# Two blocks of a transformer on one core: other splits, other places for the list steps of the experts

## The chip, the cores and the metric

The kernel runs on one core of a Trainium2 chip. The metric is the device time of one execution in microseconds (us). PE is the matrix engine, ACT the scalar engine, DVE the vector engine, POOL is GpSimd, and SP only issues transfers here.

## What is computed

512 tokens of 1024 float32 numbers pass two blocks. The first is a token mixer (mLSTM and pooled windows) followed by a mixture of 32 experts, of which each token uses four. The second is a stick-breaking attention with spatial gating. This case is about the experts:

```
gate = xb @ w_gate[e] + b_gate[e]
up = xb @ w_up[e] + b_up[e]
gate = jnp.minimum(gate, SWIGLU_LIMIT)
up = jnp.clip(up, -SWIGLU_LIMIT, SWIGLU_LIMIT)
glu = gate * jax.nn.sigmoid(SWIGLU_ALPHA * gate)
return (glu * (up + 1.0)) @ w_down[e] + b_down[e]
```

Each result row is weighted by its token's softmax gate and added to the token's output. All three weight matrices of all 32 experts are read: 96 matrices of 4 MB.

## The kernel before

**Weights.** A matrix comes in four blocks of 256 rows, 1 MB each, tile `wr` (128x2048). SP loads them (`fetch`, L132), up to eight blocks ahead of their use (`DM`). A block is then split into two tiles of the fast float32 format: ACT casts `wh` (L145), DVE subtracts `wl = wr - wh` (L148). PE multiplies with both. A block whose number stands in `k.raw` (L263) isn't split: PE multiplies `wr` itself as plain float32, which takes it more time. `next_w` keeps the instructions of the splits four blocks ahead of the product that uses them (`LEAD`).

**Places.** The experts are sorted by load at run time and stand in 32 places (`WIDE`). A wide place takes 112 rows; its activations are split into `xh` and `xl` (after the up product `ah` and `al`), which makes three products of a split block. A narrow place takes 64 rows, with both parts side by side in 128 columns (`xs`, `as`), so that two products do. The halves of a narrow result are added afterwards: ACT copies one (`part`), DVE adds (`sg`, `u`, `y`). From place 2 to 29 narrow and wide places alternate, and 30 and 31 are narrow.

**Which blocks are raw.** In gate and up of a wide place the last of four blocks; in down of every place the last. For a raw block the last 256 activations are needed unsplit: ACT copies them out of PSUM into `raws` (wide L888, narrow L900).

**Order.** In the expert stage every engine's order is the order of the Python program. `place(s)` emits gate(s), the transposes of the activations of place s-1 (`aT`, by `parts_T`), up(s), the transposes of the gathered rows of s+1 (tile `xg`), the gather for s+2 and down(s-1). So the stage repeats in pairs of places, each with one stretch of three narrow products (down N, gate N, up N) and one of three wide ones (down W, gate W, up W). Below, a block is named by product and number: D0 to D3, G0 to G3 and U0 to U3 are those of a narrow stretch.

**Steps.** Work that may be done later is a list of functions, `todo`; `product` pops one after each block. `lists` makes the token lists of four places: four marks on DVE (L800), then `rest`, 16 small matmuls into the PSUM tile `pl` (L806) and six small DVE operations. It runs at place 1 and at every fourth place to 24. Of the seven runs, six stand in a narrow stretch like that of rows 6; the other narrow stretches of the repeated part, eight, have none. Near the end `places`, `gates_T` and the bias of down are such steps too. `gates_T` copies a tile `g` on DVE (L1148) and transposes it on PE (L1151).

Of the kernel before, what the change touches and what calls it, by code (L numbers as in the profile page):

```python
# [16 lines left out]
S, D, P = 512, 1024, 128  # L17
# [229 lines left out]
def weight_order(k):  # L247

    a = k.a
    def cols(w, c0, n=512):  # L250
        kt = min(2048 // n, w.shape[0] // P)
        return [w[r:r + kt * P, c0:c0 + n].rearrange("(a p) c -> p a c", p=P) for r in range(0, w.shape[0], kt * P)]

    def rows(n, s):
        def block(r):
            def src(k):
                w = a[n][k.expert(s)]
                w = w.rearrange("e r c -> (e r) c") if s >= 2 else w
                return w[r:r + 2 * P].rearrange("(a p) c -> p a c", p=P)

            return src

        k.raw.update({len(out) + D // P // 2 - 1} if n == "w_down" or WIDE[s] else ())  # L263
        out.extend(block(r) for r in range(0, D, 2 * P))

    out = cols(a["w_in"], 1024) + cols(a["w_in"], 2048, P)
    for c0 in (512, 0, 2056, 1536):
        out += cols(a["w_in"], c0)
    for c0 in (0, 512):
        out += cols(a["w_out"], c0)[::-1]  # L270
    for e in range(NE + 1):
        if e < NE:
            rows("w_gate", e)
            rows("w_up", e)
        if e:
            rows("w_down", e - 1)
    k.experts_end = len(out)
    for cs, up in ((1024, 0, 512, 2560, 2048, 1536, 3584, 4096), "w_up_a"), ((3072, 4608, 5120), "w_up_b"):
        for c0 in cs:
            out += cols(a["w_in_2"], c0)  # L280
        for c0 in (0, 512):
            out += cols(a[up], c0)
    for c0 in (0, 512):
        out += cols(a["w_out_2"], c0)
    return out
# [503 lines left out]
    return placed  # L789


def lists(k, places, entries, name, kinds, out, soon):


    nc, n, shp = k.nc, places.shape[2], [P, NTC, P]
    oh4 = k.b4("loh" if n == 1 else "oh4", (P, n, NTC, P), BF)

    def marks(e):
        slots = k.slots[:, kinds[e], None, :].to_broadcast(shp)
        nc.vector.tensor_tensor(oh4[:, e], slots, places[:, :, e, None].to_broadcast(shp), op=OP.is_equal)  # L800

    def rest():
        pt = k.bank("pl")
        for e in range(n):
            for c in range(NTC):
                nc.tensor.matmul(pt[:, 8 * e:8 * e + 5], oh4[:, e, c], entries[:, c, e], start=(c == 0), stop=(c == NTC - 1))  # L806
        L = pt[:, :8 * n].rearrange("p (e w) -> p e w", w=8)
        tok = k.small("tok" + name, [P, n], bufs=2)
        nc.vector.tensor_reduce(tok, L[:, :, :2], axis=X, op=OP.add)
        ti, tf, ga = (k.small(t + name, [P, n], dt, bufs=3) for t, dt in (("ti", I32), ("tf", F32), ("ga", F32)))  # L810
        for kind in sorted(set(kinds)):
            for odd in range(2):
                es = [e for e in range(odd, n, 2) if kinds[e] == kind]
                if es:
                    assert es == list(range(es[0], es[-1] + 1, 2))
                    es = slice(es[0], es[-1] + 1, 2)
                    rows_of(k, tok[:, es], ti[:, es], tf[:, es], kind)
        nc.vector.tensor_reduce(ga, L[:, :, 2:5], axis=X, op=OP.add)
        out.extend((ti[:, e:e + 1], ga[:, e:e + 1], tf[:, e:e + 1]) for e in range(n))

    for e in range(n):
        soon(lambda e=e: marks(e))
    soon(rest)


# [23 lines left out]
def moe(k):  # L849
# [7 lines left out]

    info = []

    def listed(n, soon):  # L860

        s0 = max(2, listed.n)
        listed.n = s0 + n
        ss = slice(s0, s0 + n)
        lists(k, k.posm_s[:, :, ss], k.entry_s[:, :, ss], "l%d" % n, [int(not WIDE[s]) for s in range(s0, s0 + n)], info, soon)

    listed.n = 0
    ti, tf, placed = first_rows(k)
# [2 lines left out]
    k.fetch(FW)  # L871
    k.depth = 9
    bias_g, bias_u = k.bias

    def raw_part(name, parity):

# [2 lines left out]
    def parts_T(src, name, parity, wide=True):  # L879


        if wide:
            hi, lo, raw = *(k.b4(name + n, (P, KD - 2, C), F32R) for n in "hl"), raw_part(name, parity)
            def use(k0, pt):
                n = min(4, KD - 2 - k0)
                k.ondve = k.hilo(pt[:, :n], hi[:, k0:k0 + n], lo[:, k0:k0 + n])
                if n < 4:
                    nc.scalar.copy(raw, pt[:, n:])  # L888

            k.transposes(src[:C], use)  # L890
            return hi, lo, raw
        x, pt = k.b4(name + "s", (P, KD, P), F32R), k.bank("tp", (P, KD, CS))
        for kk in range(KD):
            nc.tensor.transpose(pt[:, kk], src[:CS, kk * P:(kk + 1) * P], k.ident[:CS, :CS])  # L894
        if name == "x":
            k.hilo(pt, x[:, :, :CS], x[:, :, CS:])
            return x,
        k.hilo(pt[:, :KD - 2], x[:, :KD - 2, :CS], x[:, :KD - 2, CS:])
        raw = raw_part(name, parity)[:, :, :CS]
        nc.scalar.copy(raw, pt[:, KD - 2:])  # L900
        return x, raw

    def one_of(s):
        if s < 2:
# [4 lines left out]
        nc.vector.tensor_copy(one, k.sel[:, 1:, s:s + 1].to_broadcast([96, 2, CS]))  # L909
        return one.rearrange("p a c -> p (a c)")  # L910

    todo = []

    def product(xT, b, one, get):

        wide, raw = len(xT) == 3, xT[-1] if len(xT) > 1 else None
        p, n = k.bank2("pe"), C if wide else P
        for i in range(2 if b is not None else 0):
            nc.tensor.matmul(p[:n, i], one, b[:, i * 512:(i + 1) * 512], start=True, stop=False, skip_group_check=True)  # L919
        last = KD - 3 if raw is not None else KD - 1  # L920
        for k0 in range(0, KD, 2):
            w = get()
            for i in range(2):
                kk = k0 + i
                if len(w) == 1:
                    lr = (raw[:, i], w[0]),
                elif wide:
                    lr = (xT[0][:, kk], w[0]), (xT[0][:, kk], w[1]), (xT[1][:, kk], w[0])
                else:
                    lr = (xT[0][:, kk], w[0]), (xT[0][:, kk], w[1])  # L930
                for n_, (l, r) in enumerate(lr):
                    for j in range(2):
                        o = i * D + j * 512
                        nc.tensor.matmul(p[:l.shape[1], j], l, r[:, o:o + 512], start=(b is None and kk == 0 and n_ == 0),  # L934
                                         stop=(kk in (last, KD - 1) and n_ == len(lr) - 1), skip_group_check=True)
            if todo and not k.fixed:
                todo.pop(0)()
        return p[:n].rearrange("p a b -> p (a b)")

    lim = 7.0 / (1.0 + math.exp(-1.702 * 7.0))  # L940

    def soon(f):

        f() if k.fixed else todo.append(f)

    def added(p, name):

# [114 lines left out]
    listed(2, lambda f: f())  # L1062
    gather(xgs[0], info[2][0], C if WIDE[2] else CS)

    def place(s, u, xT, one):

        if s == 1 or s % 4 == 0 and s + 4 < NE:
            listed(4, todo.append)
        sg = gate(xT, one, k.next_w)
        aT = parts_T(u, "a", (s - 1) % 2, WIDE[s - 1])  # L1070
        u = up(sg, xT, one, k.next_w)
# [4 lines left out]
            gather(xgs[s % 2], info[s + 2][0], C if WIDE[s + 2] else CS)  # L1076
        if s < NE - 1:
            result(down(aT, k.next_w), *info[s - 1][:2])
        if s == NE - 3:
            todo.extend((lambda: places(k, [info[e][2] for e in (NE - 2, NE - 1)]), lambda: gates_T(k),  # L1080
                         lambda: bias(k, "b_down", 0.0, 3)))
        return u, xT, aT, one

    k.lead, k.depth, one = LEAD, DM, one_of(1)
    with tc.manual_schedule(engines=ALL_ENGINES):
        for s in range(1, LOOP_AT + 1):
            u, xT, aT, one = place(s, u, xT, one)
        while todo:
            todo.pop(0)()
    longer_lists()  # L1090
    with tc.manual_schedule(engines=ALL_ENGINES):
        for s in range(LOOP_AT + 1, NE):
            if s == NE - 2:
                k.stop = k.experts_end
            u, xT, aT, one = place(s, u, xT, one)
        aT1 = []
        todo.append(lambda: aT1.append(parts_T(u, "a", (NE - 1) % 2, WIDE[NE - 1])))
        k.depth = DE
        p = down(aT, k.next_w)
    k.lead = 0  # L1100
    with tc.manual_schedule(engines=IN_ORDER):
        before_last(k)
        k.depth = DE2
        k.ready += [k.parts() for _ in range(4 - len(k.ready))]
        ys = [weighted(p, info[NE - 2][1])]
        p = down(aT1[0], k.next_w)
        k.wv = [k.next_w()]
        ys.append(weighted(p, info[NE - 1][1]))
        later = []
# [31 lines left out]
        nc.vector.tensor_scalar(k.ohs[:, n], iof, tf, None, op0=OP.is_equal)  # L1141


def gates_T(k):

    nc, pg, g3 = k.nc, k.bank("pg3"), k.b4("g3", (P, NTC, 96))
    k.gT3 = k.b4("gT3", (96, S), F32R)
    nc.vector.tensor_copy(g3.rearrange("p c (r e) -> p c r e", r=3),  # L1148
                          k.pg[:, :, 1, None, :].to_broadcast([P, NTC, 3, NE]))
    for c in range(NTC):  # L1150
        nc.tensor.transpose(pg[:96, c * P:(c + 1) * P], g3[:, c], k.ident)  # L1151
    nc.scalar.copy(k.gT3, pg[:96])
# [328 lines left out]
```

## Time and profile before

| | |
|---|---|
| time, median of 3 runs | 1841.8 us (1838.49 to 1843.19) |
| the profiled execution, its own time | 1837.83 us, span 1836.1 us |
| PE, DVE, ACT, POOL busy | 93%, 70%, 55%, 13% of the span |
| expert stage | about 250 to 1393 us on the trace |
| four places (two pairs) in its middle | 139.9 to 140.0 us, four times in a row |

A busy time is a sum over stages. What a stage waits for is read from the timelines of its engines, where a number in brackets is the idle time ahead of an instruction and what ended it.

### The profile page before, as it was taken

The numbers are of one execution on the slowest core, as the hardware profiler recorded it, in microseconds if no ns is written. First come the engines' busy times: TensorE is split into PE (matmuls) and PEld (weight loads), VectorE is DVE, ScalarE is ACT, GpSimd is POOL, SyncE is SP. The second block draws the span as 40 slices with busy tenths as digits, with TensorE's granted clock in tenths as the row PEclk, the third lists the DMA queues.
The fourth block names the chain that finished last, engine by engine and source line by source line (L and its number), as shares of the span: only waits on it lengthen the run. The fifth ranks groups of instructions, "written<-read, shape, count | busy, mean of one in ns | idle before, by whom it ended". The sixth has DMA issues, their size and how long they took to land.

```text
span 1836.1 us, 20169 instructions
## 1 busy us (share of the span) xinstructions
PE 1700.0 (93%) x7333; PEld 1222.6 (67%) x7333; DVE 1279.7 (70%) x1214; ACT 1018.4 (55%) x940; POOL 236.0 (13%) x211
## 2 busy tenths in 40 slices
PE   7989969989987999998998998999888999999997
PEld 5867846666664666666666666666566777777775
DVE  4766567787785887887887878878786247545352
ACT  4435345666664766765766666766674346542231
POOL 2012113101111011011011011011001100022001
PEclk9999989999998999999999999999988999999999
DMA  7225569999997999999999999999975301123241
GB/s 252 80 70 170 202 233 330 374 369 371 381 382 277 365 366 384 372 373 379 372 377 373 373 384 361 376 386 378 368 284 217 115 1 46 46 69 115 69 172 46
DMA packets 142328, 489.17 MB, mean 266 GB/s; under 512 B 10436, under 2 KB 11492, under 8 KB 142224
## 3 DMA queue, kind: packets, MB, share of 16 engines
q1 hardware_dynamic: 132176, 459.83, 66.3%
q0 software_dynamic: 8320, 21.72, 4.6%
q10 hardware_dynamic: 1728, 6.29, 0.9%
q8 instruction: 59, 0.97, 0.2%
q14 instruction: 45, 0.37, 0.1%
HBM read 474.52 MB, written 19.40 MB: 269 GB/s over the span
## 4 chain that ended last, share of the span: by engine, by line
PE 59%; DVE 5%; ACT 2%; issue 1%; POOL 1%; DMA 0%; another core or an unknown queue 0%; DVEq 0%; POOLq 0%; ACTq 0%
PE pe L934 36%; PE mm L189 5%; PE mm L190 5%; PE mm L191 5%; DVE wl L148 2%; PE pe L919 1%; PE z L1274 1%; ACT wh L145 1%; PE tp L213 1%; PE pa L1297 1%; PE tp L894 1%; PE ps L189 1%; PE ps L190 1%; PE ps L191 1%; DVE sg L950 1%
## 5 line engine op out<-in xcount | busy, mean ns | idle before, releaser
L148 DVE TENSOR_TENSOR wl<-wr,wh 128x2048 fp32r<-128x2048 f32 x365 | 826.1, 2287 | 271.1 <-ACT wh L145 230.7
L145 ACT CAST wh<-wr 128x2048 fp32r<-128x2048 f32 x365 | 681.2, 1900 | 154.3 <-PE pe L934 108.6
L934 PE MATMUL pe<-wr,raws 128*112 128x512 f32 (+1 forms) x512 | 232.6, 597 | 0.0
L934 PE MATMUL pe<-wl,xs 128*128 128x512 f32 x512 | 168.3, 411 | 15.9 <-DVE wl L148 15.9
L934 PE MATMUL pe<-wh,xs 128*128 128x512 f32 x512 | 169.1, 412 | 13.1 <-ACT wh L145 13.1
L988 POOL DMA_INDIRECT x1d<-y,til x28 | 73.8, 2634 | 830.5 <-ACT y L983 396.0
L934 PEld LDWEIGHTS pe<-wr,raws 128*112 128x112 f32 (+1 forms) x512 | 84.3, 167 | 112.9 <-issue 107.5
L934 PE MATMUL pe<-wh,xh 128*112 128x512 f32 x384 | 122.4, 400 | 10.0 <-issue 10.0
L934 PEld LDWEIGHTS pe<-wl,xs 128*128 128x128 f32 x512 | 99.9, 197 | 43.3 <-DVE wl L148 20.3
L934 PEld LDWEIGHTS pe<-wh,xs 128*128 128x128 f32 x512 | 100.2, 199 | 39.9 <-ACT wh L145 17.5
L934 PE MATMUL pe<-wl,xh 128*112 128x512 f32 x384 | 121.4, 398 | 0.0
L934 PE MATMUL pe<-wh,xl 128*112 128x512 f32 x384 | 121.0, 396 | 0.0
L190 PE MATMUL mm<-hTh,wl 128*128 128x512 f32 x296 | 117.1, 395 | 0.0
L191 PE MATMUL mm<-hTl,wh 128*128 128x512 f32 x296 | 116.8, 396 | 0.0
L189 PE MATMUL mm<-hTh,wh 128*128 128x512 f32 x296 | 115.7, 398 | 0.0
L189 PE MATMUL mm<-wh,hTh 128*128 128x512 f32 x256 | 104.0, 410 | 2.3 <-ACT v L1211 1.5
L190 PE MATMUL mm<-wh,hTl 128*128 128x512 f32 x256 | 102.5, 401 | 0.8 <-DVE hTl L185 0.8
L191 PE MATMUL mm<-wl,hTh 128*128 128x512 f32 x256 | 101.7, 399 | 0.0
L934 PEld LDWEIGHTS pe<-wh,xh 128*112 128x112 f32 x384 | 67.3, 177 | 32.7 <-issue 11.0
L934 PEld LDWEIGHTS pe<-wl,xh 128*112 128x112 f32 x384 | 67.6, 176 | 22.1
L934 PEld LDWEIGHTS pe<-wh,xl 128*112 128x112 f32 x384 | 67.5, 176 | 22.2
L888 ACT COPY raws<-tp 128x224 f32<-128x224 f32 x32 | 11.1, 346 | 118.2 <-DVE al L185 70.7
(435 smaller groups left out, 2514.0 us busy)
## 6 DMA issues: line engine op xcount, KB each, us to landing
wr<-in_w_gate SPq DMA_DIRECT2D x128, 1024.0 KB, 10.9
wr<-in_w_up SPq DMA_DIRECT2D x128, 1024.0 KB, 8.9
wr<-in_w_down SPq DMA_DIRECT2D x128, 1024.0 KB, 8.7
wr<-in_w_in SPq DMA_DIRECT2D x32, 1024.0 KB, 5.2
wr<-in_w_out SPq DMA_DIRECT2D x8, 1024.0 KB, 4.9
xt<-in_x SPq DMA_DIRECT2D x4, 512.0 KB, 10.5
x<-in_x POOLq DMA_DIRECT2D x4, 512.0 KB, 5.8
x1d<-x ACTq DMA_DIRECT2D x4, 512.0 KB, 2.8
```

Of the source, the lines that this page charges most:

```text
L145: self.nc.scalar.copy(hi[:, :n], t[:, :n])
L148: self.nc.vector.tensor_tensor(lo[:, :n], t[:, :n], f32(hi[:, :n]), op=OP.subtract)
L189: mm(ps, l[0], r[0], start=start, stop=False)
L190: mm(ps, l[1], r[0], start=False, stop=False)
L191: mm(ps, l[0], r[1], start=False, stop=stop)
L213: self.nc.tensor.transpose(pt[:, i], src[:, (k0 + i) * P:(k0 + i + 1) * P], self.ident[:n, :n])
L894: nc.tensor.transpose(pt[:, kk], src[:CS, kk * P:(kk + 1) * P], k.ident[:CS, :CS])
L919: nc.tensor.matmul(p[:n, i], one, b[:, i * 512:(i + 1) * 512], start=True, stop=False, skip_group_check=True)
L934: nc.tensor.matmul(p[:l.shape[1], j], l, r[:, o:o + 512], start=(b is None and kk == 0 and n_ == 0), stop=(kk in (last, KD - 1) and n_ == ...
L950: nc.vector.tensor_tensor(r, p[:CS], t, op=OP.add)
L988: nc.gpsimd.indirect_dma_start(out=k.x1d, out_offset=bass.IndirectOffsetOnAxis(ap=rows[:y.shape[0]], axis=0), in_=y, in_offset=None, bound ...
L1274: nc.tensor.matmul(zc[:, o:o + w], qT[rows, blk, c * P:w], kT[rows, blk, :w], start=(o == 0), stop=True, skip_group_check=True)
```

## The change

Five edits, all in the expert stage. In wide transposes the raw copy stands ahead of the split of its tile. Blocks are raw only in wide places: the last block of the 16 narrow down products is split, and the copy at L900 is gone. List steps go to a second queue, `spare`, from which `product` takes only when `todo` is empty, and four empty steps lie between the marks and `rest`. The steps near the end are put into that queue one place earlier, with `gates_T` in two parts. The last transposes (`aT1`) stand behind the down product of place 30, where they were a step within it.

```diff
-        k.raw.update({len(out) + D // P // 2 - 1} if n == "w_down" or WIDE[s] else ())
+        k.raw.update({len(out) + D // P // 2 - 1} if WIDE[s] else ())
...
     for e in range(n):
         soon(lambda e=e: marks(e))
+    for _ in range(gap):
+        soon(None)
     soon(rest)
...
                 n = min(4, KD - 2 - k0)
-                k.ondve = k.hilo(pt[:, :n], hi[:, k0:k0 + n], lo[:, k0:k0 + n])
                 if n < 4:
                     nc.scalar.copy(raw, pt[:, n:])
+                k.ondve = k.hilo(pt[:, :n], hi[:, k0:k0 + n], lo[:, k0:k0 + n])
...
-        if name == "x":
-            k.hilo(pt, x[:, :, :CS], x[:, :, CS:])
-            return x,
-        k.hilo(pt[:, :KD - 2], x[:, :KD - 2, :CS], x[:, :KD - 2, CS:])
-        raw = raw_part(name, parity)[:, :, :CS]
-        nc.scalar.copy(raw, pt[:, KD - 2:])
-        return x, raw
+        k.hilo(pt, x[:, :, :CS], x[:, :, CS:])
+        return x,
...
-            if todo and not k.fixed:
-                todo.pop(0)()
+            if (todo or spare) and not k.fixed:
+                ((todo or spare).pop(0) or int)()
...
         if s == 1 or s % 4 == 0 and s + 4 < NE:
-            listed(4, todo.append)
+            listed(4, spare.append, 4)
...
-        if s == NE - 3:
-            todo.extend((lambda: places(k, [info[e][2] for e in (NE - 2, NE - 1)]), lambda: gates_T(k),
-                         lambda: bias(k, "b_down", 0.0, 3)))
+        if s == NE - 4:
+            spare.extend((lambda: places(k, [info[e][2] for e in (NE - 2, NE - 1)]), lambda: g3.append(gates_3(k)), None,
+                          None, None, lambda: gates_T(k, g3[0]), lambda: bias(k, "b_down", 0.0, 3)))
...
-        aT1 = []
-        todo.append(lambda: aT1.append(parts_T(u, "a", (NE - 1) % 2, WIDE[NE - 1])))
         k.depth = DE
         p = down(aT, k.next_w)
-    k.lead = 0
+        k.lead = 0
+        assert not todo and not spare
+        aT1 = parts_T(u, "a", (NE - 1) % 2, WIDE[NE - 1])
```

How the order moves, at three places (`x4` is four instructions alike).

DVE, a narrow stretch with list steps, before: the splits of G0 to G2 follow the activations.

```order
L185 TENSOR_TENSOR xs<-tp,xs 128x8x64
L973 SCALAR_TENSOR_TENSOR u<-sg,u 112x1024
L148 TENSOR_TENSOR wl<-wr,wh 128x2048 x3
L987 SCALAR_TENSOR_TENSOR y<-pe,gal_4023,part 64x1024
L148 TENSOR_TENSOR wl<-wr,wh 128x2048
L800 TENSOR_TENSOR oh_6710<-slots,posm_s 128x512
L148 TENSOR_TENSOR wl<-wr,wh 128x2048
L800 TENSOR_TENSOR oh_6710<-slots,posm_s 128x512
```

And the same place of the change:

```order
L185 TENSOR_TENSOR xs<-tp,xs 128x8x64
L148 TENSOR_TENSOR wl<-wr,wh 128x2048
L970 SCALAR_TENSOR_TENSOR u<-sg,u 112x1024
L148 TENSOR_TENSOR wl<-wr,wh 128x2048 x3
L984 SCALAR_TENSOR_TENSOR y<-pe,gal_4174,part 64x1024
L148 TENSOR_TENSOR wl<-wr,wh 128x2048
L800 TENSOR_TENSOR oh_6759<-slots,posm_s 128x512
L148 TENSOR_TENSOR wl<-wr,wh 128x2048
L800 TENSOR_TENSOR oh_6759<-slots,posm_s 128x512
```

One more split, D3, stands behind `xs`; the marks stand where they stood.

ACT, the transposes of wide activations in a narrow stretch, before:

```order
L184 CAST ah<-tp 128x448
L184 CAST ah<-tp 128x224
L888 COPY raws<-tp 128x224
L145 CAST wh<-wr 128x2048
L955 ACTIVATE sg<-sg 64x1024
```

And of the change:

```order
L184 CAST ah<-tp 128x448
L895 COPY raws<-tp 128x224
L184 CAST ah<-tp 128x224
L145 CAST wh<-wr 128x2048
L952 ACTIVATE sg<-sg 64x1024
```

The raw copy moved ahead of the second cast, so that it waits for PE where it waited for DVE's `al`; the weight cast `wh` behind it is that of U3.

PE, the start of the small matmuls of a list, before: they stand behind the first block of up N.

```order
L919 MATMUL pe<-bias,one_n 128x512 x2
L934 MATMUL pe<-wh,xs 128x512 x2
L934 MATMUL pe<-wl,xs 128x512 x2
L934 MATMUL pe<-wh,xs 128x512 x2
L934 MATMUL pe<-wl,xs 128x512 x2
L806 LDWEIGHTS oh_7676
L806 MATMUL pl<-entry_s,oh_7676 128x5
```

And of the change:

```order
L935 MATMUL pe<-wh,ah 112x512 x2
L935 MATMUL pe<-wl,ah 112x512 x2
L935 MATMUL pe<-wh,al 112x512 x2
L935 MATMUL pe<-wr,raws 112x512 x4
L806 LDWEIGHTS oh_7739
L806 MATMUL pl<-entry_s,oh_7739 128x5
```

They moved behind the last block of the wide down product that follows.

## Rows read from the trace of the kernel before

**Rows 1.** The page's groups: busy us, mean ns | idle before, releaser.
```profile
L148 DVE TENSOR_TENSOR wl<-wr,wh 128x2048 fp32r<-128x2048 f32 x365 | 826.1, 2287 | 271.1 <-ACT wh L145 230.7
```

**Rows 2.** Windows (start:end us): length, busy times, PEclk, DMA share, GB/s.
```profile
759.06:898.97 139.91, 132.08 (x553) 90.38 (x552) 114.04 (x79) 92.98 (x70) 18.50 (x8) 0.98 0.99 375
...
1246.98:1308.00 61.02, 58.05 (x234) 38.39 (x233) 48.38 (x32) 39.97 (x30) 6.68 (x3) 1.00 1.01 389
```

**Rows 3.** Timeline of PE, no list: start, duration, [idle before <-releaser].
```profile
738.25 0.71 PE L894 MATMUL tp<-ident,xg 64*128 64x64 f32 x8
...
744.65 3.65 PE L934 MATMUL pe<-wr,raws 128*64 128x512 f32 x8
748.23 0.73 PE L919 MATMUL pe<-bias,one_n 96*128 96x512 f32 x2
...
764.50 0.77 PE L934 MATMUL pe<-wh,xs 128*128 128x512 f32 x2 [1.32 <-ACT wh L145]
766.82 0.74 PE L934 MATMUL pe<-wl,xs 128*128 128x512 f32 x2 [1.56 <-DVE wl L148]
...
767.87 0.62 PE L934 MATMUL pe<-wl,xs 128*128 128x512 f32 x2
768.33 0.93 PE L213 MATMUL tp<-ident,xg 112*128 112x112 f32 x8
```

**Rows 4.** Timeline of DVE, the same pair.
```profile
739.91 0.68 DVE L185 TENSOR_TENSOR xs<-tp,xs 128x512 fp32r<-128x512 f32 x1
...
749.48 1.28 DVE L987 SCALAR_TENSOR_TENSOR y<-pe,gal,part 64x1024 f32<-64x1024 f32 x1 [0.27 <-ACT part L986]
751.41 8.90 DVE L148 TENSOR_TENSOR wl<-wr,wh 128x2048 fp32r<-128x2048 f32 x4 [0.65 <-ACT wh L145]
760.23 1.21 DVE L950 TENSOR_TENSOR sg<-pe,part 64x1024 f32<-64x1024 f32 x1
761.37 0.90 DVE L185 TENSOR_TENSOR al<-tp,ah 128x448 fp32r<-128x448 f32 x2
764.48 2.29 DVE L148 TENSOR_TENSOR wl<-wr,wh 128x2048 fp32r<-128x2048 f32 x1 [2.21 <-ACT wh L145]
```

**Rows 5.** Timeline of ACT, the same pair.
```profile
738.99 0.59 ACT L184 CAST xs<-tp 128x512 fp32r<-128x512 f32 x1 [2.59 <-PE tp L894]
...
762.30 0.34 ACT L888 COPY raws<-tp 128x224 f32<-128x224 f32 x1 [3.79 <-DVE al L185]
762.54 1.90 ACT L145 CAST wh<-wr 128x2048 fp32r<-128x2048 f32 x1
```

**Rows 6.** Timeline of PE, a pair with list steps.
```profile
806.33 0.71 PE L894 MATMUL tp<-ident,xg 64*128 64x64 f32 x8
...
832.49 0.57 PE L806 MATMUL pl<-entry_s,oh 128*128 128x5 bf16 x16 [4.96 <-DVE al L185]
...
833.92 1.05 PE L934 MATMUL pe<-wl,xs 128*128 128x512 f32 x2
...
840.25 0.93 PE L213 MATMUL tp<-ident,xg 112*128 112x112 f32 x8
```

**Rows 7.** Timeline of DVE in that pair: the last mark.
```profile
830.10 0.68 DVE L800 TENSOR_TENSOR oh<-slots,posm_s 128x512 bf16<-128x512 f32 x1
```

**Rows 8.** Timeline of PE, the last places.
```profile
1294.24 0.71 PE L894 MATMUL tp<-ident,xg 64*128 64x64 f32 x8
...
1313.51 1.09 PE L1151 MATMUL pg<-ident,g 128*96 128x128 f32 x4 [4.81 <-DVE g L1148]
...
1330.48 0.74 PE L934 MATMUL pe<-wl,xs 128*128 128x512 f32 x2 [1.59 <-DVE wl L148]
...
1332.49 1.11 PE L894 MATMUL tp<-ident,xg 64*128 64x64 f32 x8
...
1378.01 0.71 PE L894 MATMUL tp<-ident,u 64*128 64x64 f32 x8 [3.52 <-DVE u L973]
```

**Rows 9.** Timeline of ACT, the last places.
```profile
1318.67 1.05 ACT L617 CAST bias<-braw 96x1024 fp32r<-96x1024 f32 x1 [1.66 <-DMA braw<-in_b_down]
```

More of the change, by code (lines that the diff above doesn't have):

```diff
@@ L789, in rows_of, with lists @@
     return placed
-def lists(k, places, entries, name, kinds, out, soon):
+def lists(k, places, entries, name, kinds, out, soon, gap=0):
     nc, n, shp = k.nc, places.shape[2], [P, NTC, P]
@@ L858, in moe, with listed @@
     info = []
-    def listed(n, soon):
+    def listed(n, soon, gap=0):
         s0 = max(2, listed.n)
@@ L864, in listed @@
         ss = slice(s0, s0 + n)
-        lists(k, k.posm_s[:, :, ss], k.entry_s[:, :, ss], "l%d" % n, [int(not WIDE[s]) for s in range(s0, s0 + n)], info, soon)
+        lists(k, k.posm_s[:, :, ss], k.entry_s[:, :, ss], "l%d" % n, [int(not WIDE[s]) for s in range(s0, s0 + n)], info, soon, gap)
     listed.n = 0
@@ L873, in moe, with soon @@
     bias_g, bias_u = k.bias
+    todo, spare = [], []
+    def soon(f):
+        todo.append(f) if k.lead and not k.fixed else f()
     def raw_part(name, parity):
@@ L910, in one_of @@
         return one.rearrange("p a c -> p (a c)")
-    todo = []
     def product(xT, b, one, get):
-        wide, raw = len(xT) == 3, xT[-1] if len(xT) > 1 else None
+        wide = len(xT) == 3
         p, n = k.bank2("pe"), C if wide else P
@@ L919, in product @@
             nc.tensor.matmul(p[:n, i], one, b[:, i * 512:(i + 1) * 512], start=True, stop=False, skip_group_check=True)
-        last = KD - 3 if raw is not None else KD - 1
+        last = KD - 3 if wide else KD - 1
         for k0 in range(0, KD, 2):
@@ L925, in product @@
                 if len(w) == 1:
-                    lr = (raw[:, i], w[0]),
+                    lr = (xT[2][:, i], w[0]),
                 elif wide:
@@ L935, in product @@
                                          stop=(kk in (last, KD - 1) and n_ == len(lr) - 1), skip_group_check=True)
-            if todo and not k.fixed:
-                todo.pop(0)()
+            if (todo or spare) and not k.fixed:
+                ((todo or spare).pop(0) or int)()
         return p[:n].rearrange("p a b -> p (a b)")
     lim = 7.0 / (1.0 + math.exp(-1.702 * 7.0))
-    def soon(f):
-        f() if k.fixed else todo.append(f)
     def added(p, name):
@@ L1063, in moe @@
     gather(xgs[0], info[2][0], C if WIDE[2] else CS)
+    g3 = []
     def place(s, u, xT, one):
         if s == 1 or s % 4 == 0 and s + 4 < NE:
-            listed(4, todo.append)
+            listed(4, spare.append, 4)
         sg = gate(xT, one, k.next_w)
@@ L1087, in moe @@
             u, xT, aT, one = place(s, u, xT, one)
-        while todo:
-            todo.pop(0)()
+        for f in todo + spare:
+            (f or int)()
+        todo.clear()
+        spare.clear()
     longer_lists()
@@ L1105, in moe @@
         ys = [weighted(p, info[NE - 2][1])]
-        p = down(aT1[0], k.next_w)
+        p = down(aT1, k.next_w)
         k.wv = [k.next_w()]
@@ L1141, in places, with gates_3, gates_T @@
         nc.vector.tensor_scalar(k.ohs[:, n], iof, tf, None, op0=OP.is_equal)
-def gates_T(k):
-    nc, pg, g3 = k.nc, k.bank("pg3"), k.b4("g3", (P, NTC, 96))
+def gates_3(k):
+    g3 = k.b4("g3", (P, NTC, 96))
+    k.nc.vector.tensor_copy(g3.rearrange("p c (r e) -> p c r e", r=3),
+                            k.pg[:, :, 1, None, :].to_broadcast([P, NTC, 3, NE]))
+    return g3
+def gates_T(k, g3):
+    nc, pg = k.nc, k.bank("pg3")
     k.gT3 = k.b4("gT3", (96, S), F32R)
-    nc.vector.tensor_copy(g3.rearrange("p c (r e) -> p c r e", r=3),
-                          k.pg[:, :, 1, None, :].to_broadcast([P, NTC, 3, NE]))
     for c in range(NTC):
```

## The prediction

> **What bounds the kernel now.** I read the windows of the expert stage first, then the timelines of its engines, since the page's shares mix stages. Two pairs of places take 139.91 us, of which PE is busy 132.08, DVE 114.04 and ACT 92.98 [rows 2]. So PE sets the pace, and it idles 7.8 us in four places. The timeline says where.
>
> In a narrow stretch without list steps PE waits 1.32 us for a cast and 1.56 for the subtraction behind it, both of U3 [rows 3]. The chain reads backwards: `wl` of U3 starts at 764.48 after 2.21 us without work on DVE [rows 4], its cast `wh` on ACT at 762.54, right behind `raws`, which stood 3.79 us for DVE's `al` [rows 5], and `al` ended at 762.27 behind four subtractions and `sg` [rows 4]. So ACT and DVE wait for each other in turn, and PE for both.
>
> In a stretch with list steps the wait is another: PE stands 4.96 us ahead of the small matmuls [rows 6]. The releaser named is again `al`, since `pl` takes a PSUM bank that `al` still reads; four marks of .68 us, .61 without the overlap of .07, make DVE that much later [rows 7]. Behind the wait a pair of matmuls takes 1.05 us where one takes .62 [rows 3, 6]: the granted clock has fallen from the 2.4 to the 1.2 GHz level. Four such pairs run so, and 1.7 us are lost.
>
> Weights are no wait: ACT's casts there wait for engines, not for landings. But the DMA share is .99 [rows 2], a rival below.
>
> **The change, part by part.** I time a narrow stretch from its first transposes T (738.25) to the transposes that end up N (768.33): 30.08 us [rows 3].
>
> *What PE saves.* A raw narrow block costs 3.58 us (3.65 less .07 of overlap) [rows 3]; split it is four pairs of matmuls at .46 (767.87 to 768.33), 1.86. That is -1.72. Without the waits of 2.88 the stretch would need 30.08 - 2.88 - 1.72 = 25.5 us. The raw copy ahead of `ah` takes DVE out of ACT's wait, at no cost: it was .34 us in either place [rows 5].
>
> *What DVE pays.* One more subtraction in the same stretch, twelve where eleven were, and it is DVE that I take to set the new end. ACT's cast of `xs` ends at 738.99 + .59, T + 1.33 [rows 5]. The new cast of D3 stands right behind it, 1.90 us like that of rows 5, so DVE can start on D3 at T + 3.25. From there its order has no work to wait for until U3: D3, the `u` operation, G0 to G2, `y`, G3, U0 to U2, `sg`, `al`, U3. One subtraction alone takes 2.287 [rows 1]; back to back they start 2.205 apart (four took 751.41 to 760.23, 8.82) [rows 4], and nine are 19.85; `sg` to the next start 1.14, `u` the same by its like size, `y` 1.21 (its 1.28 less .07), `al` .83 [rows 4]: 24.2 us in all. U3 is split at T + 27.4. Three pairs of matmuls follow, 1.51 us (766.82 to 768.33) [rows 3], so up N ends at T + 28.9. On the way PE meets G3 late too: its `wl` is ready at T + 16.6, PE asks for it near T + 14.9. So the stretch has a wait of about 1.7 us for G3 and one of about 2.0 for U3, 3.7 in place of 2.9, and still gains 30.08 - 28.9 = **1.2 us**. Eight such stretches: **-9.6**. This is the main step: two thirds of what PE could save go to DVE.
>
> *List stretches.* The marks stay where they were on DVE, four times .61 [rows 7], so U3 is split at T + 29.8 and up N ends at T + 31.3. The small matmuls, .57 us [rows 6], now run behind the wide down, long after `al`, and their DVE operations in the wide stretch, where DVE has slack. So T + 31.9 against 33.92 (806.33 to 840.25) [rows 6]: **-2.0** each if PE keeps its clock. The waits are then some .7 us at U1, 1.0 at U2 and 2.9 at U3, near the 4.96 that cost the clock before, but in three parts. If it falls, 1.7 comes back and -.3 is left. Six stretches: -12 or **-1.8**.
>
> *The last places.* The narrow stretch from 1294.24 to 1332.49 took 38.25 us, with a wait of 4.81 for `g` at its small transposes and half clock behind it [rows 8]. These steps leave it for the wide place before, so it costs 28.9 like the others: **-9.3**. At its end the clock fell (transposes of 1.11 us instead of .71 [rows 3, 8]), after a wait of 1.59; if that goes too it is 2.6 more. Against it: ACT's cast of the down bias stands behind a transfer that ended its wait of 1.66 us before [rows 9]. It is issued on POOL behind the scatter of a `y` and now has another cover; nothing earlier than that row prices it, so 0 to 4 us, of which I take 2. At the very end nothing is won: D3 and the last `as` are split, the transposes behind down of 30 wait for `u` as they did (3.52 us [rows 8]), and DVE's `as` has two more subtractions ahead of it than the operation that preceded, 4.4 us, while two raw blocks less give back 3.4. Tail: **-7.3**, from -5.3 to -11.9.
>
> *Sum.* With the clock falling in every list stretch -9.6 - 1.8 - 7.3 = -18.7; with none falling -9.6 - 12 - 11.9 = -33.5. I take the middle, -26, because the three waits are each shorter than the one that dropped the clock. The profiled execution took 1837.83 us, 4.0 under the median of the runs, so about 1812 for such an execution and **1816** against the median. Differences within 0.3%, 5.5 us, this measurement can't tell from no change.
>
> **The rivals.**
>
> *DVE keeps up, and transfers set the end.* If DVE started D3 earlier than T + 3.25, the stretch would fall towards 25.5 us and the pairs be worth 4.6 each without lists and 8.4 with them, 87 in all with PE never waiting. Then weights come next: at the best rate seen over a long stretch, 389 GB/s (61.02 us at a DMA share of 1.01), the bytes that now go at 375 need 139.91 x 375 / 389 = 134.9 us [rows 2]. That is -5.0 for four places, -36 over the seven such units of the stage, and with the tail -44: 1798. For it: ACT idles 2.59 us ahead of `xs` [rows 5]. Against it: the new order puts the cast of D3 behind `xs`.
>
> *Transfers are the bound already.* The DMA share is .99 [rows 2]; were 375 GB/s all there is, PE's waits would only move to the landings, and the tail alone would gain: 1834. Against it: the same queue moved 389 for 61 us in rows 2. The Trainium skill, DMA: Bandwidth & Descriptors, section "Where 436 GB/s comes from", has a rule that speaks for this rival: for transfers between HBM and SBUF a limit of about 358 GB/s per core binds. By that rule the kernel already runs above its limit and nothing could be gained; the trace disagrees, with 375 and 389. The same page's section "Measured" has 425 for a core whose neighbour is idle, by which the floor of four places would be, as an estimate, 123 us.
>
> *The clock falls in each narrow stretch.* This is the slower end. The new waits of 1.7 and 2.0 us are longer than the 1.32 and 1.56 that left the clock alone [rows 3], and a wait of 1.59 like the latter did cost it once [rows 8]. One fall in each of 14 stretches at 1.7 leaves 8 x (+.5) - 1.8 - 7.3 = -5: 1837. Two falls in each, at G3 and at U3, add 14 x 1.7 = 24: +19, 1861. It decides from a loss of 33.5 / 14 = 2.4 us for each stretch on. Against two falls: the waits of G3 and U3 lie some 10 us apart, and the one long wait of before cost one fall.
>
> **How the numbers follow.** The DVE-bound forecast has .60, transfers as the new bound .13, transfers as the old bound .05, one fall in each stretch .14, two falls .08. Faster by over 0.3% are the first two, half of the third and some of the fourth: .78; within it .14; slower .08. The range leaves out the two falls and the far end of the fast rival: 1790 to 1838.
>
> **What would show it.** Right: in a narrow stretch PE waits at G3 and at U3 for `wl`, with DVE without idle time from D3 to U3, and a stretch of 28.5 to 29.5 us; no wait at the small matmuls; `raws` on ACT released by PE; 136 to 138 us for four places, at 380 to 385 GB/s. Wrong: casts that wait for landings; a wait of PE below 1 us in all; PEclk below .95 in the windows; a bias cast on ACT that waits over 4 us.

## The result, and the profile after

The changed kernel takes 1811.91 us (median of 4 runs, 1807.62 to 1822.25) against 1840.14 for the kernel before: ratio 0.9855, 95% interval 0.9808 to 0.9902, or 27 us less by the ratio, where 1816 was forecast. Its profiled execution is the slowest of the four, 1822.25 us with a mean granted clock of .971; the other three have .977 to .980 and 1814 to 1808. So the trace shows 15.6 us of gain between the two profiled executions (1837.83 and 1822.25 us). Most of the rest of the 27 lies in executions of the changed kernel that kept more of their clock; some 2 us come from the profiled execution of the kernel before, which is that much under its median.

DVE of the changed kernel in the narrow stretch that answers to [rows 4]; this one begins at T = 729.84:

```profile
733.02 2.29 DVE L148 TENSOR_TENSOR wl<-wr,wh 128x2048 fp32r<-128x2048 f32 x1 [0.87 <-ACT wh L145]
735.23 1.22 DVE L970 SCALAR_TENSOR_TENSOR u<-sg,u 112x1024 f32<-112x1024 f32 x1
736.36 6.69 DVE L148 TENSOR_TENSOR wl<-wr,wh 128x2048 fp32r<-128x2048 f32 x3
742.97 1.27 DVE L984 SCALAR_TENSOR_TENSOR y<-pe,gal,part 64x1024 f32<-64x1024 f32 x1
744.16 8.88 DVE L148 TENSOR_TENSOR wl<-wr,wh 128x2048 fp32r<-128x2048 f32 x4
752.97 1.21 DVE L947 TENSOR_TENSOR sg<-pe,part 64x1024 f32<-64x1024 f32 x1
754.10 0.90 DVE L185 TENSOR_TENSOR al<-tp,ah 128x448 fp32r<-128x448 f32 x2
754.93 8.88 DVE L148 TENSOR_TENSOR wl<-wr,wh 128x2048 fp32r<-128x2048 f32 x4
```

Behind the first row no bracket stands: DVE works without a pause from D3 through U3 (the first of the last four subtractions, 754.93 to about 757.13) into the wide stretch. That is T + 3.2 to T + 27.3, where the forecast had T + 3.25 to T + 27.4.

ACT in the same stretch, for [rows 5]:

```profile
731.08 7.31 ACT L145 CAST wh<-wr 128x2048 fp32r<-128x2048 f32 x4
...
749.73 0.35 ACT L895 COPY raws<-tp 128x224 f32<-128x224 f32 x1
...
750.20 1.93 ACT L145 CAST wh<-wr 128x2048 fp32r<-128x2048 f32 x1
```

The bracket of 3.79 <-DVE al ahead of `raws` is gone, and the cast of U3 follows at 750.20, well ahead of its use. It is the subtraction alone that is late now.

PE in the same stretch, for [rows 3]:

```profile
729.84 0.71 PE L902 MATMUL tp<-ident,xg 64*128 64x64 f32 x8
...
746.49 0.73 PE L935 MATMUL pe<-wl,xs 128*128 128x512 f32 x2 [1.26 <-DVE wl L148]
...
757.26 1.03 PE L935 MATMUL pe<-wl,xs 128*128 128x512 f32 x2 [1.86 <-DVE wl L148]
758.08 1.06 PE L935 MATMUL pe<-wh,xs 128*128 128x512 f32 x2
...
759.79 1.49 PE L213 MATMUL tp<-ident,xg 112*128 112x112 f32 x8
```

Two waits stand in brackets, both for `wl`, as forecast: 1.26 us at G3 (1.7 forecast; G1 and G2 are late by .1 and .2 before it) and 1.86 at U3 (2.0). Behind the second the granted clock falls to the 1.2 GHz level: pairs of 1.03 and 1.06 us, transposes of 1.49 us instead of .93. So up N ends at T + 29.95 instead of T + 28.9, and .1 of the 1.2 us is left. In the stretches from 440.66 and 591.67 us the waits were the same, the clock stayed, and up N ended at T + 28.9 as forecast.

PE in a list stretch, for [rows 6]:

```profile
798.27 0.71 PE L902 MATMUL tp<-ident,xg 64*128 64x64 f32 x8
...
828.09 0.74 PE L935 MATMUL pe<-wl,xs 128*128 128x512 f32 x2 [2.64 <-DVE wl L148]
...
829.91 1.70 PE L213 MATMUL tp<-ident,xg 112*128 112x112 f32 x8
```

No wait at the small matmuls any more. U3's `wl` comes at T + 29.8, to the tenth as forecast, and up N ends at T + 31.6 with the clock falling right at its end.

The windows of four places, for [rows 2], an early one and a later one:

```profile
608.27:746.47 138.20, 129.94 (x552) 90.94 (x552) 118.01 (x81) 96.56 (x71) 35.06 (x9) 0.99 1.00 377
...
886.19:1025.90 139.71, 131.47 (x552) 92.25 (x552) 117.96 (x81) 96.64 (x70) 33.94 (x9) 0.98 0.99 375
```

PEclk is the granted clock as a share of the full one. The first window holds one fall of the clock, behind the list stretch (.99, 138.2 us); the second holds two, one behind a stretch without lists and one behind a list stretch (.98, 139.7 us), and there the profiled execution gains almost nothing over the 139.91 of before.

PE in the last places, for [rows 8]:

```profile
1286.32 0.71 PE L902 MATMUL tp<-ident,xg 64*128 64x64 f32 x8
...
1314.65 0.73 PE L935 MATMUL pe<-wl,xs 128*128 128x512 f32 x2 [1.84 <-DVE wl L148]
...
1316.24 0.71 PE L902 MATMUL tp<-ident,xg 64*128 64x64 f32 x8
...
1358.83 0.71 PE L902 MATMUL tp<-ident,u 64*128 64x64 f32 x8 [2.27 <-DVE u L970]
1363.84 1.22 PE L935 MATMUL pe<-wh,as 128*128 128x512 f32 x2 [4.29 <-DVE as L185]
```

The last narrow stretch ahead of a wide product takes 29.92 us (1286.32 to 1316.24) where it took 38.25, with no wait for `g`.

Windows from the end of the last expert product to the end of the program, before and after:

```profile
1393.24:1836.10 442.86, 419.02 (x1897) 325.97 (x1896) 213.14 (x198) 166.98 (x199) 41.40 (x58) 0.98 0.23 78
```

```profile
1373.45:1820.40 446.95, 422.39 (x1897) 327.88 (x1895) 212.60 (x198) 166.98 (x199) 41.39 (x58) 0.97 0.23 77
```

No edit lies there, and it is 4.1 us longer at a lower clock. Over all the kernels of this document this part took 442.0 to 449.2 us, the longest where PEclk was .96, the shortest where it was .99.

### The profile page after: what moved, and what is told of

Its sections match the earlier page's. It is cut to its first block, busy times and chain, and to the rows that moved or that the text cites. A ratio compares the mean times of both kernels' runs of the same rounds, so it can differ in the third digit from the quotient of the medians.

```text
span 1820.4 us, 20173 instructions
## 1 busy us (share of the span) xinstructions
PE 1683.7 (92%) x7333; PEld 1231.3 (68%) x7333; DVE 1310.5 (72%) x1230; ACT 1046.7 (57%) x940; POOL 345.3 (19%) x211
## 4 chain that ended last, share of the span: by engine, by line
PE 54%; DVE 11%; issue 2%; ACT 1%; another core or an unknown queue 1%; POOL 0%; DVEq 0%; POOLq 0%; ACTq 0%
PE pe L935 30%; DVE wl L148 8%; PE mm L189 5%; PE mm L190 5%; PE mm L191 5%; PE tp L213 1%; PE z L1281 1%; PE pa L1304 1%; PE pe L920 1%; PE ps L189 1%; PE tp L902 1%; PE ps L190 1%; PE ps L191 1%; DVE sg L947 1%
## 5 line engine op out<-in xcount | busy, mean ns | idle before, releaser
L148 DVE TENSOR_TENSOR wl<-wr,wh 128x2048 fp32r<-128x2048 f32 x381 | 859.5, 2280 | 223.4 <-ACT wh L145 183.2
L145 ACT CAST wh<-wr 128x2048 fp32r<-128x2048 f32 x381 | 713.7, 1903 | 203.8 <-PE pe L935 139.2
L985 POOL DMA_INDIRECT x1d<-y,til x28 | 177.3, 6332 | 708.5 <-DVE y L984 453.1
L935 PE MATMUL pe<-wl,xs 128*128 128x512 f32 x512 | 172.0, 418 | 58.1 <-DVE wl L148 56.9
L935 PE MATMUL pe<-wr,raws 128*112 128x512 f32 x384 | 172.6, 592 | 0.0
L935 PEld LDWEIGHTS pe<-wl,xs 128*128 128x128 f32 x512 | 92.7, 192 | 105.3 <-DVE wl L148 88.6
L935 PE MATMUL pe<-wh,xs 128*128 128x512 f32 x512 | 162.2, 398 | 0.0
L935 PEld LDWEIGHTS pe<-wr,raws 128*112 128x112 f32 x384 | 67.8, 176 | 78.1 <-issue 72.7
L935 PE MATMUL pe<-wh,as 128*128 128x512 f32 x256 | 82.9, 405 | 4.3 <-DVE as L185 4.3
L935 PE MATMUL pe<-wl,as 128*128 128x512 f32 x256 | 81.2, 399 | 1.7 <-DVE wl L148 1.5
```

The costliest lines, as they stand in the source:

```text
L145: self.nc.scalar.copy(hi[:, :n], t[:, :n])
L148: self.nc.vector.tensor_tensor(lo[:, :n], t[:, :n], f32(hi[:, :n]), op=OP.subtract)
L985: nc.gpsimd.indirect_dma_start(out=k.x1d, out_offset=bass.IndirectOffsetOnAxis(ap=rows[:y.shape[0]], axis=0), in_=y, in_offset=None, bound ...
```

## Experiments

The first four share their runs of the kernel before, so do the next four and the last three; kernels of different groups are compared by their ratios to these.

**The raw copy first, alone (x1).** The kernel before with this edit:

```diff
-                k.ondve = k.hilo(pt[:, :n], hi[:, k0:k0 + n], lo[:, k0:k0 + n])
                 if n < 4:
                     nc.scalar.copy(raw, pt[:, n:])
+                k.ondve = k.hilo(pt[:, :n], hi[:, k0:k0 + n], lo[:, k0:k0 + n])
```

> The kernel before with one edit alone: in wide transposes the raw copy ahead of the split. Theory (DVE's queue sets the end of a narrow stretch): the cast of U3 no longer waits for al, so its subtraction follows al at once (762.27 to 764.48 instead of 764.48 to 766.69); PE waits .9 us there instead of 2.9, eight stretches and the last places gain 2.0 each, list stretches nothing since PE still stands for the small matmuls: -14 to -18 us against the kernel before. Rival (the raw copy was not what held ACT): no change within 5 us.

Measured: 1815.43 us, ratio 0.9843 (0.9814 to 0.9871), -29 us. One moved line has the worth of the whole change. PE at U3, timeline, a stretch without lists:

```profile
755.92 0.74 PE L934 MATMUL pe<-wl,xs 128*128 128x512 f32 x2 [0.90 <-DVE wl L148]
```

.90 us of wait, as expected, where it was 1.32 and 1.56. The size was under-expected. In the profiled execution the eight stretches without lists took 27.8 us instead of 30.05, 2.3 less each with no fall of the clock, the last narrow one 35.6 instead of 38.25, and the list stretches gained nothing. All in all it is 19.6 us shorter than the profiled execution of before, although the part behind the experts, which no edit touches, took 5.2 us more at a lower clock. The rest of the difference of medians, 27.4, is that x1's profiled execution lies 2.8 above its median and that of before 5.0 under the median of the runs beside x1.

**The split alone (x2).** The kernel before with the last block of narrow down products split:

```diff
-        k.raw.update({len(out) + D // P // 2 - 1} if n == "w_down" or WIDE[s] else ())
+        k.raw.update({len(out) + D // P // 2 - 1} if WIDE[s] else ())
...
-        if name == "x":
-            k.hilo(pt, x[:, :, :CS], x[:, :, CS:])
-            return x,
...
+        k.hilo(pt, x[:, :, :CS], x[:, :, CS:])
+        return x,
```

> The kernel before with one edit alone: the last block of narrow down products split. Theory: PE saves 1.72 us in each of 16 places but DVE has 2.2 us more in the same stretch, with the wait between ACT and DVE still there, so a stretch without lists ends about 1 us later and one with lists about where it did: +3 to +12 us against the kernel before. Rival (PE sets the pace, the split pays): 16 x 1.7 = -27 us.

Measured: 1862.68 us, ratio 1.0104 (1.0081 to 1.0127), +19 us: slower, by more than expected. PE at U3:

```profile
777.47 0.73 PE L929 MATMUL pe<-wh,xs 128*128 128x512 f32 x2 [2.29 <-ACT wh L145]
779.79 1.11 PE L929 MATMUL pe<-wl,xs 128*128 128x512 f32 x2 [1.59 <-DVE wl L148]
...
782.41 1.39 PE L213 MATMUL tp<-ident,xg 112*128 112x112 f32 x8
```

Waits of 2.29 and 1.59 in place of 1.32 and 1.56, and now the clock falls behind them: a pair of 1.11, transposes of 1.39. The stretch, from 750.08 to 782.41, takes 32.3 us where it took 30.08. PE's saving of 27 us is lost and more.

**The list queue alone (x3).** The kernel before with:

```diff
+    for _ in range(gap):
+        soon(None)
     soon(rest)
...
-            if todo and not k.fixed:
-                todo.pop(0)()
+            if (todo or spare) and not k.fixed:
+                ((todo or spare).pop(0) or int)()
...
-            listed(4, todo.append)
+            listed(4, spare.append, 4)
...
```

> The kernel before with one edit alone: list steps in a second queue with four empty steps ahead of the small matmuls. Theory: the wait of 4.96 us and the half clock behind it go, but the marks stay in DVE's queue and U3 waits for them: a list stretch ends at T + 32.3 and the small matmuls follow, 1.0 us gained in each of six: -4 to -8 us against the kernel before. Rival (the whole wait and the clock come back): 6 x 6.6 = -40 us.

Measured: 1847.67 us, ratio 1.0029 (1.0003 to 1.0054). A miss: no gain. PE at U3 of a list stretch:

```profile
837.53 0.73 PE L936 MATMUL pe<-wh,xs 128*128 128x512 f32 x2 [3.07 <-ACT wh L145]
839.86 1.22 PE L936 MATMUL pe<-wl,xs 128*128 128x512 f32 x2 [1.59 <-DVE wl L148]
...
843.96 1.18 PE L936 MATMUL pe<-wh,ah 128*112 128x512 f32 x2
```

The wait of 4.96 is gone from the small matmuls and back at U3 as 3.07 and 1.59, since the four marks still stand ahead of U3 on DVE. The clock falls behind it too: rows of 1.18 us at 843.96 are in the wide down product. In this execution it also fell in three of the eight stretches without lists, behind the same 1.3 and 1.6 us of waits that had left it alone before.

**The change without the split (x4).** The changed kernel with the last block of narrow down products raw again:

```diff
-        k.raw.update({len(out) + D // P // 2 - 1} if WIDE[s] else ())
+        k.raw.update({len(out) + D // P // 2 - 1} if n == "w_down" or WIDE[s] else ())
...
+        raw = raw_part(name, parity)[:, :, :CS]
+        nc.scalar.copy(raw, pt[:, KD - 2:])
+        k.hilo(pt[:, :KD - 2], x[:, :KD - 2, :CS], x[:, :KD - 2, CS:])
+        return x, raw
...
```

> The changed kernel without one edit: the last block of narrow down products is raw again. Theory (in the narrow stretch DVE sets the end): one subtraction less in DVE's chain, U3 split at T + 26.2 and up N ended at T + 27.7 instead of 29.2; list stretches 1.1 earlier, fewer falls of the clock: 15 to 30 us faster than the changed kernel, about 1790, although PE has 27 us more work. Rival (PE sets the pace): 16 x 1.7 = 27 us slower than the changed kernel, 1839.

Measured: 1795.32 us, ratio 0.9740 (0.9714 to 0.9767), 17 us faster than the changed kernel by medians, 21 by ratio. PE in a narrow stretch:

```profile
726.48 0.71 PE L902 MATMUL tp<-ident,xg 64*128 64x64 f32 x8
...
732.86 3.65 PE L940 MATMUL pe<-wr,raws 128*64 128x512 f32 x8
...
752.73 0.73 PE L940 MATMUL pe<-wl,xs 128*128 128x512 f32 x2 [0.90 <-DVE wl L148]
...
754.22 0.93 PE L213 MATMUL tp<-ident,xg 112*128 112x112 f32 x8
```

The raw block takes its 3.65 us again, and yet up N ends at T + 27.74 (726.48 to 754.22), not 28.9 as in the changed kernel with its clock up or 29.95 as in the stretch shown above, behind a fall. This tells the two theories apart: a kernel in which PE has 27 us more to do is faster, because DVE has one subtraction less in the stretch. The wait of .90 left the clock alone in all eight stretches without lists, so part of the gain is the clock. (The narrow raw copy stands ahead of its split here, where it stood behind it before; x1, without that, has the same 27.75.)

**Splits five blocks ahead (y1)** and its control **(z3)**, both on the changed kernel; z3 keeps LEAD at 3:

```diff
-LEAD, DM = 3, 8
+LEAD, DM = 4, 6
```

> The changed kernel with splits emitted five blocks ahead instead of four (LEAD 4), and to make room six weight blocks loaded ahead instead of eight (DM 6). Theory (DVE's queue in the narrow stretch sets its end, and DVE has slack in the wide one): every subtraction starts a block earlier, U3 is split near T + 25.2, PE's waits of 1.3 and 1.9 shrink below .5 and the clock stays up: 25 to 40 us faster than the changed kernel's 1812. Rival (transfers are the bound, at a DMA share of .99): casts wait for landings, and the time is within 6 us of 1812 or slower.

Measured: 1792.14 us, ratio 0.9726 (0.9704 to 0.9747), 24 us under the changed kernel by ratio, just under what was expected. A window of four places:

```profile
616.10:749.40 133.30, 128.32 (x552) 89.58 (x552) 117.50 (x81) 95.80 (x71) 43.09 (x9) 1.00 1.03 394
```

PEclk is 1.00, and what DVE couldn't do in the narrow stretch it did in the wide one ahead: the narrow stretch without lists from 720.91 takes 26.0 us, and PE now waits 1.04 us for `wl` early in the wide ones. From about 850 us on casts wait for landings too, which none does in the changed kernel, but the next eight places stay at 133.4 and 133.5 us for four.

> The changed kernel with six weight blocks loaded ahead instead of eight and nothing else, as the control for y1. Theory (loads land well before their use, and what helped y1 is DVE starting earlier): within 4 us of 1812. Rival (fewer transfers in flight are what helped): 15 us or more faster than 1812.

Measured: 1808.15 us, ratio 0.9827 (0.9793 to 0.9860), its interval overlapping that of the change and clear of that of y1. It is the earlier start of DVE that helps. Four places in it:

```profile
595.10:731.60 136.50, 128.27 (x554) 89.65 (x553) 117.82 (x80) 95.45 (x70) 38.17 (x8) 1.00 1.00 377
```

PE's waits are those of the changed kernel (1.26 at G3, 1.84 at U3, 2.65 in list stretches), and yet the clock stayed up behind them in ten narrow stretches in a row, from 512 to 1170 us of this execution.

**The wait filled (y2).** The changed kernel with products by zero ahead of the late rows:

```diff
...
+                    for q in range(2 * fill if n_ == 1 else 0):
+                        nc.tensor.matmul(p[:P, q % 2], k.zer.to_broadcast([P, P]), w[0][:, (q % 2) * 512:(q % 2) * 512 + 512], start=False,
+                                         stop=False, skip_group_check=True)
```

> The changed kernel with matmuls by zeros put where PE waits in a narrow stretch: two pairs ahead of the wl rows of G3, three ahead of those of U3, .9 and 1.4 us of waits of 1.3 and 1.9. They add zeros to the sum, so the result is the same. Theory (half of what the change costs beside DVE is the clock that falls after the wait for U3): PEclk 1.00 through the stage, 1.7 us back per fall, 5 to 15 us faster than 1812. Rival (falls cost nothing, since DVE sets the end anyway): within 4 us of 1812.

Measured: 1805.51 us (1803.73 to 1810.0), ratio 0.9802 (0.9780 to 0.9823), 6 us under the changed kernel by medians and 10 by ratio; the two intervals overlap, so the worth isn't shown clear of noise. A window of four places:

```profile
609.20:745.70 136.50, 132.93 (x572) 93.52 (x572) 118.02 (x81) 96.45 (x70) 36.12 (x9) 1.00 1.01 382
```

Nothing was taken from DVE; PE only had something to do while it waited, and the clock stayed: PEclk 1.00, 136.5 us, where the forecast for no falls gives 139.9 - 1.2 - 2.0 = 136.7. That the products by zero kept it up isn't shown by one execution, since z3 held 136.5 us without them; for it speaks that no narrow stretch of this execution lost its clock, and that all five runs lie within 7 us, where the six of z3 spread over 1803 to 1822.

**The marks in the wide stretch (y3).** x4 with:

```diff
+    for _ in range(8 if gap else 0):
+        soon(None)
     for e in range(n):
         soon(lambda e=e: marks(e))
```

> The kernel with raw narrow blocks (x4, 1795) with eight empty steps ahead of the four marks as well, so that the marks run in the wide stretch. Theory: DVE's chain to U3 in the six list stretches is 2.4 us shorter, so PE waits .9 us there as in the others: 12 to 16 us faster than x4, about 1781. Rival (the marks only take DVE's time elsewhere): within 4 us of x4.

Measured: 1786.8 us, ratio 0.9703 (0.9681 to 0.9725), 7 to 9 us under x4 (the intervals overlap a little), the fastest of all by its median. Four places, and the largest of ACT's waits for a landing between 600 and 1250 us (us in total, times, longest):

```profile
619.00:750.80 131.80, 129.97 (x553) 89.44 (x553) 113.59 (x79) 93.19 (x71) 16.24 (x8) 1.00 1.02 392
```

```profile
ACT wh L145 <- DMA wr<-in_w_down: 16.3, 13, 3.5
```

The rate is 392 GB/s, and from 1020 us on casts wait for weights, which they did nowhere in this stretch of the kernel before. PE waits .9 us in the list stretches as expected, and between the profiled executions of x4 and y3 the six pairs of places with list steps gain 17.6 us, more than expected. The whole gains less because of both ends of the stage: at 334 us PE waits 3.24 us for `gal` of the first lists, which now come too late (4.9 us lost in that pair), and in the last pair and the last places 7.0 us are lost, where casts wait for landings.

**The late steps put back (y4).** The changed kernel with:

```diff
-        if s == NE - 4:
-            spare.extend((lambda: places(k, [info[e][2] for e in (NE - 2, NE - 1)]), lambda: g3.append(gates_3(k)), None,
-                          None, None, lambda: gates_T(k, g3[0]), lambda: bias(k, "b_down", 0.0, 3)))
+        if s == NE - 3:
+            todo.extend((lambda: places(k, [info[e][2] for e in (NE - 2, NE - 1)]), lambda: gates_T(k, gates_3(k)),
+                         lambda: bias(k, "b_down", 0.0, 3)))
```

> The changed kernel with the steps near the end (places, gates_T whole, the bias of down) put back one place later, into todo, as before the change; the other edits stay. Theory: PE stands again some 4.8 us for g in the last narrow stretch, with a fall of the clock behind it: 5 to 10 us slower than 1812. Rival (the last stretch is set by DVE's subtractions in any case): within 3 us of 1812.

Measured: 1824.55 us, ratio 0.9891 (0.9870 to 0.9913), 7 us slower by ratio and 13 by medians; its interval overlaps that of the change. PE in the last narrow stretch:

```profile
1306.83 1.09 PE L1158 MATMUL pg<-ident,g 128*96 128x128 f32 x4 [9.67 <-DVE g L1148]
```

The wait for `g` is back, and longer than the 4.81 of before: PE comes 1.7 us earlier, since D3 is split, and `g` 3.1 us later, 2.2 of which are the one subtraction more that DVE has ahead of it. The stretch itself (1284.44 to 1322.34) takes 37.90 us against 29.92.

**All of it together (z1, z2).** z1 is y3 with LEAD, DM = 4, 6; z2 is y1 with the marks of y3.

> y3 (raw narrow blocks, marks in the wide stretch, 1787) with splits five blocks ahead and six weight blocks loaded ahead. Theory (PE's last waits in the stage are .9 us for U3 in each pair): they go, four places fall from 131.7 to about 130 and the time by 10 to 14 us, to about 1775. Rival (at 392 GB/s and a DMA share of 1.02 transfers now bound it): within 4 us of 1787, with casts or products that wait for landings, or slower.

> y1 (the changed kernel with splits five ahead, 1792) with the marks in the wide stretch. Theory: three waits of .7 and one of .6 us go from each list stretch, four places fall from 133.3 to about 130.7, and the time to about 1774. If transfers don't bind it, it comes out no slower than the same with raw narrow blocks, since PE has 1.7 us less in each pair. Rival (transfers bind at 392 GB/s, 131.7 us for four places): 1780 or more.

Measured: z1 1793.37 us, ratio 0.9740 (0.9718 to 0.9762); z2 1793.81, ratio 0.9740 (0.9719 to 0.9762). Neither gains on what it was made from, and the two agree although PE and DVE have different work in them. ACT's waits for landings in z1, 600 to 1250 us, and two windows of four places:

```profile
ACT wh L145 <- DMA wr<-in_w_gate: 53.3, 45, 3.2
ACT wh L145 <- DMA wr<-in_w_down: 49.3, 23, 6.8
...
ACT wh L145 <- DMA wr<-in_w_up: 33.0, 32, 2.8
```

```profile
719.36:848.46 129.10, 129.10 (x555) 89.40 (x552) 111.06 (x78) 93.35 (x70) 32.47 (x8) 1.00 1.02 395
...
877.70:1012.80 135.10, 132.45 (x553) 88.47 (x553) 113.25 (x79) 93.88 (x71) 30.18 (x9) 1.00 1.01 390
```

135.6 us of waits for weights at 100 casts. Until about 850 us z1 does what was expected and better: four places in 129.1 us, PE without idle time. That used up loads made ahead (as an estimate, rate times length, 51 MB were moved in that window, where four places of before moved 52.5); then casts wait, and four places take 133.6 to 135.1 us at 389 to 393 GB/s and a DMA share of 1.01 to 1.02. From there on transfers are the bound, with six loads ahead as here; eight loads ahead with splits five blocks ahead weren't run, so that the number of loads ahead has a part in it isn't excluded.

## Why the prediction was right, and where not

**The bound.** Right, and shown from three sides. The chain from D3 to U3 ran as worked out, to about a tenth of a microsecond; taking a subtraction out of it (x4) made the kernel faster against 27 us more work on PE; starting it earlier (y1) did too.

**The edits taken apart.** Here the prediction was blunt. It summed the narrow stretch as a whole, -1.2 us, and wrote that two thirds of what PE could save go to DVE; the raw copy was called an edit without cost. x1, x2 and x4 show that the raw copy alone brings as much as the whole change, that lists and last places bring another 19 us on top of it (x1 to x4, by ratio), and that the split takes 17 to 21 us away. The chain held the answer: without D3 the same addition ends at T + 27.7, which x4 then measured as 27.74. I never worked the stretch with one edit and not the other.

**The clock.** The sum had two ends, -33.5 us without a fall and -18.7 with one in every list stretch, and took the middle. y2's profiled execution, which lost no clock in the narrow stretches, measures the first end, since its fillers leave DVE's chain alone: against the profiled execution of before, -9.2 in the pairs of places without lists (-9.6 forecast), -12.7 in those with lists (-12), -11.4 from the last narrow stretch through the last expert product (-11.9 at best). In the profiled execution of the changed kernel the same three are -2.1, -4.4 and -11.9, with 4.1 lost to the clock behind the experts. There the clock fell in every narrow stretch from 689 to 1249 us, with or without lists, and a fall cost about 1.6 us (those pairs of places against the same in y2). This is the rival of one fall in each stretch, and where it holds the gain is nearly nothing, 139.7 against 139.91 us. Other executions of the same kernel kept more of the clock. So the terms were right, but that the middle, -26, came out so near the measured 27 is partly luck: its reason, that shorter waits in three parts spare the clock in the list stretches, failed in five of the six here, and five of the eight stretches without lists, taken as safe in the main forecast, lost it too.

**List stretches.** Chain right (T + 29.8). x3 shows that the queue alone is worth nothing, and with the raw copy first it pays: from x1 to x4, ratio .9843 to .9740, the profiled executions gain 12.6 us in the pairs with lists and 8.5 in the last places. No run has the last transposes moved by themselves.

**The last places.** -7.3 forecast. The trace gives -8.3 for the last narrow stretch (-9.3 forecast) and -3.5 from there to the end of the last expert product, since the clock didn't fall at its end (the forecast gave 2.6 for that, as its better case). The wide place before it, to which the steps went, took 1.3 us more, 1.0 of it a fall of the clock: y2, with its clock up, has .3 there. The 2 us that the forecast put on the wait of the bias cast were nothing, as that cast waits for no landing now. y4 prices the move of the steps: 8.0 us in the stretch.

**Signs.** The waits, DVE's unbroken chain and the raw copy without its wait for DVE came as written. Four places of 136 to 138 us at 380 to 385 GB/s did not in this execution (138.2 at 377, 139.7 at 375): they hold with the clock up, 136.5 at 382 in y2.

**Transfers.** The rival of transfers as the bound already is refuted: four places ran at 382 to 394 GB/s in y1 to y3. The other rival had its bound right: 389 GB/s and 134.9 us, worked out from rows of before, stand against 390 and 135.1 in the later part of z1. The 131.8 us of y3 are no pace that transfers could keep: as an estimate from rates and lengths of windows, it moved 206 MB for sixteen places (592.76 to 1119.69 us) where the kernel before moved 209, and so used up loads made ahead until its casts waited. By the limit of about 358 GB/s that the Trainium skill, DMA: Bandwidth & Descriptors, section "Where 436 GB/s comes from", gives for such transfers, none of these rates could have been measured; the trace disagrees with it.

## What to carry to other kernels

When an edit moves work from the engine that seems to set the pace to another, add up the other's queue over the very stretch in which it is late, with the edit and without. Work out each edit of a bundle alone: here one moved line won 29 us and a larger edit gave 17 to 21 back. A wait that can't be shortened may still be worth filling for the sake of the clock; the runs here speak for it but don't settle it. And a window that beats the pace of transfers may only be using up what was loaded ahead.

## What the runs showed of the hardware

The clock is a matter of the single execution. Four runs of the changed kernel gave 1807.62, 1809.83, 1813.99 and 1822.25 us at mean granted clocks of .980, .979, .977 and .971; with the wait filled five lay within 1804 to 1810 at .979 to .984. Waits of 1.3 and 1.6 us in a row left it alone in the eight narrow stretches without lists of before and cost it in three of the eight in x3. One of 1.86 cost it at 757 us of the changed kernel and in the narrow stretches after up to 1247 us, but waits of 1.85 us at 468 and 619 did not, nor did ten waits of 1.8 to 2.7 us in z3 between 540 and 1170 us.

Loads into this one core held 389 to 393 GB/s over 400 us of z1 with casts waiting for them, and that is where two kernels with different work on PE and DVE met.
